# Attention's conversions and normalisation held in the source's order, row maxima transposed on VectorE, a fifth buffer of queries, and 44 expert groups in place of 46

## The chip, the cores and the metric

The kernel runs on one core of a Trainium2 chip. The metric is the device time of one launch in microseconds (us). A core has TensorE (PE; its weight loads are listed as PEld), VectorE (DVE), ScalarE (ACT), GpSimd (POOL) and SyncE (SP), which here only issues DMAs. Each engine takes its instructions in the order in which they stand in its stream. That order is not the order of the source: a planner chooses it before the program is built, by its own estimate of when each input is there, unless the source ties an instruction to the one before it on its engine.

## The reference

Two layers, 2048 tokens, width 1024. Each layer is a mixer, a layer norm, a mixture of experts and a layer norm. The first mixer is causal attention with 16 heads, whose scores have a part with 64 columns and a rotated part with 32; the second is a pooling mixer. Cut to what matters:

```
s = (q_nope @ k_nope.T + q_rope @ k_rope.T) * scale      # 16 heads, 64 + 32 columns
p = softmax(where(causal, s, -inf));  o = p @ v;  f = o @ w_o
x = layer_norm(alpha * x + f)
# experts: 64, two of them for each token, chosen within one of 8 groups
e = two of 64 per token, with gates
y[t] = sum over its two e of gate * (silu(x[t] @ w1[e]) * (x[t] @ w3[e])) @ w2[e]
x = layer_norm(alpha * x + y)
```

All is float32. The 4096 choices (two for each token) fall unevenly on the 64 experts.

## The kernel before

The stages follow each other: projections (queries, keys and values go to DRAM), attention, output projection with norm and routing, experts of layer 0, the pooling mixer with norm and routing, experts of layer 1, the last norm.

Attention works on pairs of heads `hp` (8) and blocks `b` of 512 queries (4). `run` goes through the steps (hp, b, k), k being a chunk of 128 keys: 40 steps for each pair of heads, two to a round, so 20 rounds. In a round stand, in this order: the scores of two steps (`scores`: ten matmuls for each into a PSUM tile `sc`, of which there are two; on the diagonal a mask added by VectorE at L906; then the exponential `pe` on ScalarE at L908), one item of maxima, the sums of the round before (`add`, one head on VectorE at L921, one on GpSimd at L922), the product with the values (`apply`, tile `po`), the steps of unfinished normalisations, a second item of maxima.

The maxima (`maxima`) run 24 items ahead of the scores. An item is four matmuls into the single PSUM tile `pm`, on the diagonal a mask on VectorE (L817), and a VectorE maximum (L819). After the last item of a (hp, b) the 128 x 8 maxima are turned by a TensorE transpose (L836) into a tile `sc`, negated by VectorE (L838), written to DRAM (`M`) and read from there into one row of each head's `qb` (two DMAs). The scores' matmuls add that row.

`finish` normalises a finished (hp, b): sums over the keys by a matmul into `sc`, two ScalarE copies `rl` and `o` (L865, L866), then through DRAM: sums out (L868), back as 128 x 8 (L871), reciprocal on VectorE (L874), out (L875), back spread over partitions (L878), product on GpSimd (L881), a split of `o` into two float32r halves `ot` (ScalarE L193, GpSimd L194), and a DMA to `OT` (L887). Each yield in it is one round.

`load_queries` brings a block of queries (one DMA for `qn`, L790, four for `qb`, L794) and splits both into two halves with `split` (ScalarE L193, GpSimd L194), after two ends of rounds (`behind`, `round`). There are four buffers of queries. `all_maxima` loads the next block when the maxima of one begin. `load_pair` brings keys (L776) and values.

`pin` ties an instruction behind the one that was traced before it on its engine. Before the change it is used for attention's matmuls, its masks, its maxima and VectorE's part of the sums. The exponentials, GpSimd's part of the sums, the splits, the copies of `finish`, the reciprocal and the DMAs are left to the planner.

The experts: a group is 128 rows in four blocks of 32 rows, each block of one expert. `groups` lays out which place (experts ranked by how many rows they have) gets how many blocks: 6 for places 0 to 2, 4 for 3 to 12, 3 for 13 to 36, 2 for 37 to 63, in all 46 groups, and `WORK` is their order. Rows over an expert's seats go to a loop at the end (`overflow`), run only when there are such rows. For each group a gather brings the rows, TensorE turns them (L1352), multiplies by w1 and w3 (L1364) and w2 (L1392), and a scatter writes them. The three matrices of an expert are 3 MB; `load_line` brings them on SP in the order of first use into five (layer 0) or six (layer 1) buffers, three of them during the stage before.

Of the kernel before, what the change touches and what calls it, by code (L numbers as in the profile page):

```python
# [20 lines left out]
P = 128  # L21
# [10 lines left out]
AT4, AT3, AT2 = 3, 13, 37  # L32
# [9 lines left out]
FIRST_AT = 6  # L42
LATE = -4
# [26 lines left out]
def groups():  # L70
# [3 lines left out]
    rests = [[(p, 4), (p, 5), (AT2 + p, 0), (AT2 + p, 1)] for p in range(AT4)]  # L74
    line = [(p, q) for p in range(AT3, AT2) for q in range(3)]
    threes = [line[i:i + NQ] for i in range(0, len(line), NQ)]
    line = [(p, q) for p in range(AT2 + AT4, NE) for q in range(2)]
# [5 lines left out]
    big = [[g] for g in range(n[1], n[2])] + [[g, n[2] + g] for g in range(n[1])]  # L83
    mid = [[g, g + 1, g + 2] for g in range(n[3], n[4], 3)]
    small = [[g] for g in range(n[4], n[5])]
    work = mid.pop(0)
    for i in range(len(big)):
# [3 lines left out]
    work += [g for part in (mid, small) for x in part for g in x]  # L91
    assert sorted(work) == list(range(len(every)))
# [10 lines left out]
def block_runs():  # L103
# [5 lines left out]
    for g, blocks in enumerate(GROUPS):  # L109
        for j, (p, q) in enumerate(blocks):  # L110
            kind = next(i for i, end in enumerate((AT3, AT2, AT2 + AT4, NE)) if p < end)
            found.setdefault((kind, j, q), []).append((p, g))
# [564 lines left out]
class Attention:  # L677


    def __init__(self, tc, c, QN, QR, K, KR, V, M, R, OT):  # L680
# [6 lines left out]
        self.acc, self.later, self.tails = {}, [], []  # L687
        self.ps = None
# [7 lines left out]
    def matmul(self, *a, **kw):  # L696
        return self.pin(self.nc.tensor.matmul(*a, **kw))  # L697

# [17 lines left out]
    def begin(self):  # L716
# [17 lines left out]
        for j in range(2):  # L734
            nc.gpsimd.memset(self.kb[j * DN + DR:j * DN + DR + 1].bitcast(F32), 1.0)
        self.new_keys(p0, 0)
        self.load_queries(0, 0)
        for b in range(NB - 1):
            self.load_pair(0, b)
            yield  # L740
            for _ in range(4 * (b + 1)):
                self.next_maxima()
# [7 lines left out]
    def load_rotated(self, b):  # L750
# [3 lines left out]
        raw = self.p0.tile([P, TB], F32, name="kraw")  # L754
# [3 lines left out]
        nc.gpsimd.tensor_tensor(raw, raw, self.ka[:, tb].bitcast(F32), op=ALU.subtract)  # L758
# [6 lines left out]
    def load_pair(self, hp, b):  # L765
# [11 lines left out]
        self.behind(lambda: split(nc, kt[:, 0, tb], kt[:, 1, tb], raw, nc.gpsimd))  # L777
# [3 lines left out]
    def load_queries(self, hp, b):  # L781
# [3 lines left out]
        qn = self.pq.tile([P, 2, TB], F32R, name="qn", bufs=4)  # L785
        qa = self.pq.tile([P, TB], F32R, name="qa", bufs=4)
        qb = self.pq.tile([P, TB], F32R, name="qb", bufs=4)
# [3 lines left out]
        self.behind(lambda: split(nc, qn[:, 0], qn[:, 1], raw, nc.gpsimd))  # L791
# [3 lines left out]
        self.behind(lambda: split(nc, qa, qb, rot, nc.gpsimd))  # L795

    def maxima(self, hp, b):
# [8 lines left out]
        for tt in range(4):  # L806
            for ch in range(b + 1):
# [18 lines left out]
    def next_maxima(self):  # L826
        tails, self.tails = self.tails, []
        next(self.maxima_of_all, None)
        for x in tails:
            x()  # L830

    def maxima_row(self, hp, b, mc):
        nc = self.nc
        qb = self.qs[hp, b][2]
        pt = (self.ps or self.psm).tile([P, 2, TB], F32, name="sc" if self.ps else "pm")[:, 0]
        self.pin(nc.tensor.transpose(pt[:8, :P], mc.rearrange("p j t -> p (j t)"), self.c.ident))  # L836
        mr = self.pq.tile([8, P], F32R, name="mr")
        self.pin(nc.vector.tensor_scalar(mr, pt[:8, :P], -1.0, None, op0=ALU.mult))  # L838
        nc.sync.dma_start(self.M[hp, b], mr.bitcast(F32))
        self.ready.add((hp, b))  # L840
        for j in range(2):
            r = j * DN + DR
            nc.sync.dma_start(qb[r:r + 1].bitcast(F32), self.M[hp, b, 4 * j:4 * j + 4].rearrange("t p -> (t p)").unsqueeze(0))

    def all_maxima(self):
        for i, x in enumerate(self.order):
            if 0 < i + 1 < len(self.order) and self.order[i + 1] != (0, NB - 1):
# [867 lines left out]
```

## Time and profile before

| | us |
|---|---|
| median of 3 runs (2955.05 to 2965.54) | 2963.32 |
| profiled execution, its own time | 2968.73 |
| span of its trace | 2966.5 |
| attention with maxima and scores alone, 375 to 1197 | 822 |
| experts of layer 0, 1447 to 2050 | 603 |
| experts of layer 1, 2282 to 2851 | 569 |

The projections end inside the first pairs of heads, so the stretch from 375 on is attention alone. In the page and in the trace's answers a group has the busy time and then the idle time of its engine just before it, with what ended that idle time. An arrow `<-` names the releaser.

### The profile page before, as it was taken

What the parts mean: (1) busy time and instruction counts of PE and PEld (TensorE: products, weight loads), DVE (VectorE), ACT (ScalarE), POOL (GpSimd) and SP (SyncE); (2) the same over time, 40 slices, a digit from 0 to 9 for tenths busy, and PEclk for the clock granted to TensorE, in tenths of its full rate; (3) what the DMA queues carried; (4) which work ended last, traced back from release to release, by engine and by line L of the source; (5) the groups of instructions that cost most, each with busy time, mean ns of one, the idle gap of its engine ahead of it and who ended that gap; (6) DMA issues with size and microseconds to landing.
All of it is one profiled execution on the core that took longest, in us unless ns stands there. A gap on an engine that the chain in (4) does not pass through costs nothing.

```text
span 2966.5 us, 50666 instructions
## 1 busy us (share of the span) xinstructions
PE 2657.1 (90%) x19378; PEld 1482.6 (50%) x19378; DVE 1454.7 (49%) x3675; ACT 823.2 (28%) x1433; POOL 897.4 (30%) x831
## 2 busy tenths in 40 slices
PE   6987989889898899999799999896996999999977
PEld 5874555555455555688533334332895333333323
DVE  7555767677677776455421111221896211111218
ACT  4444434434444434222111111111552111111102
POOL 4244656656565556200111111111111111111100
PEclk9998999999999999999899999998997999999988
DMA  6545122121221211647599999996756899999967
GB/s 202 194 154 172 55 65 80 58 72 55 80 65 55 72 37 56 190 147 240 194 385 418 409 415 403 370 419 217 209 174 272 334 419 417 412 412 412 414 259 291
DMA packets 230241, 690.21 MB, mean 233 GB/s; under 512 B 42318, under 2 KB 102990, under 8 KB 180588
## 3 DMA queue, kind: packets, MB, share of 16 engines
q1 hardware_dynamic: 189180, 577.62, 51.3%
q0 software_dynamic: 29408, 78.29, 7.8%
q10 hardware_dynamic: 11408, 31.02, 2.7%
q8 instruction: 155, 2.54, 0.3%
q14 instruction: 90, 0.74, 0.1%
HBM read 595.47 MB, written 120.71 MB: 241 GB/s over the span
## 4 chain that ended last, share of the span: by engine, by line
PE 57%; DMA 23%; DVE 12%; issue 3%; ACT 2%; POOL 1%; SPq 0%; ACTq 0%; DVEq 0%; POOLq 0%; another core or an unknown queue 0%
DMA w<-in_w_dram 15%; PE ph L1364 14%; PE sc L697 9%; PE po L697 6%; PE py L1392 6%; PE pz L1103 6%; PE pm L697 5%; DVE mx L819 3%; PE pt L1352 2%; PE pt L387 2%; PE pl L344 2%; PE plog L520 1%; PE pz L1244 1%; DMA R<-rl 1%; DMA qn<-QN 1%
## 5 line engine op out<-in xcount | busy, mean ns | idle before, releaser
L1364 PE MATMUL ph<-w,xT 128*32 128x512 f32 x5888 | 681.2, 602 | 39.3 <-DMA w<-in_w_dram 39.3
L1364 PEld LDWEIGHTS ph<-w,xT 128*32 128x32 f32 x5888 | 199.7, 111 | 447.6 <-issue 432.1
L819 DVE TENSOR_REDUCE mx<-pm 128x2 f32<-128x1024 f32 (+2 forms) x320 | 339.5, 1061 | 108.0 <-PE pm L697 102.7
L908 ACT ACTIVATE pe<-sc 128x1024 f32<-128x1024 f32 (+1 forms) x320 | 280.0, 895 | 367.1 <-DVE sc L906 211.0
L922 POOL TENSOR_TENSOR acc<-acc,pe 128x512 f32<-128x512 f32 (+3 forms) x256 | 311.8, 1218 | 218.5 <-ACT pe L908 210.2
L1321 POOL DMA_INDIRECT Y<-y,idst x92 | 92.3, 1003 | 936.7 <-ACT xT L1353 874.3
L1369 DVE SCALAR_TENSOR_TENSOR h<-sg,gate,ph 128x256 f32<-128x256 f32 x92 | 44.2, 481 | 657.5 <-ACT sg L1367 657.5
L1392 PE MATMUL py<-w,hT 128*32 128x512 f32 x2944 | 348.8, 592 | 1.6 <-DVE hT L1379 1.6
L697 PE MATMUL po<-pe,vt 128*64 128x512 f32 (+3 forms) x1280 | 283.0, 565 | 0.0
L697 PE MATMUL sc<-qn,k 64*128 64x512 f32 (+2 forms) x1920 | 260.5, 377 | 19.7 <-ACT rl L865 15.7
L921 DVE TENSOR_TENSOR acc<-acc,pe 128x512 f32<-128x512 f32 (+3 forms) x256 | 236.9, 925 | 11.0 <-ACT pe L908 10.0
L1367 ACT ACTIVATE sg<-ph 128x256 f32<-128x256 f32 x92 | 35.3, 383 | 719.3 <-PE ph L1364 707.2
L1392 PEld LDWEIGHTS py<-w,hT 128*32 128x32 f32 x2944 | 106.5, 110 | 214.2 <-issue 214.1
L697 PE MATMUL pm<-k,qn 64*128 64x512 f32 (+2 forms) x640 | 147.5, 454 | 71.2 <-DVE mx L819 65.3
L697 PEld LDWEIGHTS sc<-qn,k 64*128 64x128 f32 x1920 | 176.9, 194 | 65.3 <-ACT rl L865 20.9
L1394 DVE COPY y<-py 128x512 f32<-128x512 f32 x92 | 63.6, 692 | 224.4 <-PE py L1392 224.4
L697 PEld LDWEIGHTS pm<-k,qn 64*128 64x128 f32 x640 | 65.3, 196 | 192.4 <-DVE mx L819 97.7
L697 PEld LDWEIGHTS po<-pe,vt 128*64 128x64 f32 x1280 | 81.2, 142 | 134.7 <-issue 126.2
L1352 PEld LDWEIGHTS pt<-ident,xg 128*128 128x128 f32 x736 | 90.4, 194 | 97.9 <-issue 72.9
L1352 PE MATMUL pt<-ident,xg 128*128 128x128 f32 x736 | 108.3, 291 | 23.7 <-DMA xg<-X,isrc 22.4
L697 PE MATMUL pm<-ka,qa 64*128 64x512 f32 (+2 forms) x640 | 125.3, 383 | 0.3 <-ACT qa L193 0.3
L697 PE MATMUL sc<-qb,kb 33*128 33x512 f32 (+2 forms) x640 | 121.8, 372 | 0.0
(360 smaller groups left out, 4082.5 us busy)
## 6 DMA issues: line engine op xcount, KB each, us to landing
w<-in_w_dram SPq DMA_DIRECT2D x384, 1024.0 KB
fy<-Y SPq DMA_DIRECT2D x16, 1024.0 KB
OT<-ot SPq DMA_DIRECT2D x31, 512.0 KB
K<-kq SPq DMA_DIRECT2D x32, 256.0 KB
V<-v SPq DMA_DIRECT2D x16, 512.0 KB
QN<-kq SPq DMA_DIRECT2D x32, 256.0 KB
qn<-QN SPq DMA_DIRECT2D x32, 256.0 KB
qb<-QR SPq DMA_DIRECT2D x128, 64.0 KB
```

Source lines behind the costliest of these rows:

```text
L344: nc.tensor.matmul(pl, a[:, k, :], w[:, k, :], start=(k == 0 and n == 0), stop=(k == ND - 1 and n == 2))
L697: return self.pin(self.nc.tensor.matmul(*a, **kw))
L819: self.pin(nc.vector.tensor_reduce(mx[:, :, tt, ch], pm[:, :, :n], axis=AX.X, op=ALU.max))
L908: nc.scalar.activation(pe[:, :, c0:], sc[:, :, c0:], AF.Exp, scale=SCALE)
L921: self.pin(self.nc.vector.tensor_tensor(acc[:, 0, c0:], before[:, 0, c0:], pe[:, 0, c0:], op=ALU.add))
L922: self.nc.gpsimd.tensor_tensor(acc[:, 1, c0:], before[:, 1, c0:], pe[:, 1, c0:], op=ALU.add)
L1103: nc.tensor.matmul(pz, o[:, a, k, :], wo.parts[k][b][:, hs], start=(n == 0), stop=(n == 3 * ND - 1))
L1321: st = self.nc.gpsimd.indirect_dma_start(out=self.Y, out_offset=bass.IndirectOffsetOnAxis(ap=idx, axis=0), in_=y, in_offset=None, bounds_c ...
L1352: self.pin(nc.tensor.transpose(pt[:, j, :], x[:, half * 4 + j, :], self.c.ident))
L1364: self.pin(nc.tensor.matmul(ph[js], xT[:, k, js], w[:, :, k, :], start=(k == 0), stop=(k == ND - 1), tile_position=(0, j * n)))
L1392: self.pin(nc.tensor.matmul(py[js], hT[:, k, js], w[:, k, hs], start=(k == 0), stop=(k == NF - 1), tile_position=(0, j * n)))
L1394: (nc.vector.tensor_copy if half else nc.scalar.copy)(y[:, hs], py)
```

## The change

- In attention, the splits, the copies, the reciprocal and the product of `finish` are pinned too (`split` of the class, L865, L866, L874, L881). The exponentials, GpSimd's part of the sums and all DMAs are not.
- The maxima are no longer turned on TensorE. VectorE negates them into eight columns of a 128 x 32 tile and transposes that in 32 x 32 blocks; eight DMAs of 4 x 32 elements for each (hp, b) write the rows of `qb` straight from SBUF. The DRAM tile `M` is no longer used. The step `next_maxima`, which did the turning one item later, goes.
- A fifth buffer of queries (in the pool `p1`, for every fifth block), and each block from the second pair of heads on is loaded eight items of maxima ahead of its first use.
- `finish` keeps `o` in the second half of `ot`, with three buffers of `ot` and none of `o`. The rotated keys are loaded into the place of the split keys in place of a tile of their own.
- The experts' places get 6 blocks (place 0), 5 (1 and 2), 4 (3 to 12), 3 (13 to 34), 2 (35 to 59) and 1 (60 to 63): 44 groups. `WORK` starts with the same four groups; the experts with the most rows come at the 5th, 8th and 14th group in place of the 34th, 40th and 42nd; the last group holds the last two places.

```diff
-AT4, AT3, AT2 = 3, 13, 37
+AT5, AT4, AT3, AT2, AT1 = 1, 3, 13, 35, 60
+AHEAD = 8
...
+    def split(self, hi, lo, src):
+        self.pin(self.nc.scalar.copy(hi, src))
+        self.pin(self.nc.gpsimd.tensor_tensor(lo, src, hi.bitcast(F32), op=ALU.subtract))
...
-        self.behind(lambda: split(nc, kt[:, 0, tb], kt[:, 1, tb], raw, nc.gpsimd))
+        self.behind(lambda: self.split(kt[:, 0, tb], kt[:, 1, tb], raw))
...
+        pool, bufs = (self.p1, 1) if self.order.index((hp, b)) % 5 == 4 else (self.pq, 4)
...
-                    self.tails.append(lambda: self.maxima_row(hp, b, mc))
+                    mr, mt = self.mr, self.pq.tile([P, 32], F32R, name="mt")
+                    self.pin(nc.vector.tensor_scalar(mr[:, 0:8], mc.rearrange("p j t -> p (j t)"), -1.0, None, op0=ALU.mult))
+                    self.pin(nc.vector.transpose(mt.bitcast(F32), mr.bitcast(F32)))
+                    self.ready.add((hp, b))
+                    for j in range(2):
+                        row = qb[j * DN + DR:j * DN + DR + 1].rearrange("o (t q c) -> o t q c", t=4, q=4)
+                        for q in range(4):
+                            e = 32 * q + 4 * j
+                            nc.sync.dma_start(row[:, :, q].bitcast(F32), mt[e:e + 4].bitcast(F32))
...
+            for _ in self.maxima(*x):
+                while waiting and items >= waiting[0][0]:
+                    self.load_queries(*waiting.pop(0)[1])
+                items += 1
+                yield
...
-            nc.scalar.copy(rl, pl)
-            nc.scalar.copy(o, po)
+            self.pin(nc.scalar.copy(rl, pl))
+            self.pin(nc.scalar.copy(o, po))
...
-            nc.vector.reciprocal(r8, r8)
+            self.pin(nc.vector.reciprocal(r8, r8))
...
-            nc.gpsimd.tensor_tensor(o, o, rl, op=ALU.mult)
+            self.pin(nc.gpsimd.tensor_tensor(o, o, rl, op=ALU.mult))
```

## Rows read from the trace of the kernel before

**Rows 1.** The page's first part: busy time, share of the span and instructions of each engine.

```profile
PE 2657.1 (90%) x19378; PEld 1482.6 (50%) x19378; DVE 1454.7 (49%) x3675; ACT 823.2 (28%) x1433; POOL 897.4 (30%) x831
```

**Rows 2.** Busy time by stage: the stretch, its length, busy time of each engine with its instructions, then the granted clock, the DMAs' share and GB/s. Attention, the experts of layer 0, the experts of layer 1.

```profile
375.00:1197.00 822.00, 730.18 (x5160) 425.89 (x5156) 586.67 (x817) 336.24 (x443) 493.83 (x413) 0.95 0.21 63
...
1447.00:2050.00 603.00, 565.27 (x4943) 215.10 (x4943) 122.59 (x265) 73.52 (x140) 95.35 (x108) 0.96 0.93 379
2282.00:2851.00 569.00, 542.64 (x4755) 200.91 (x4755) 101.56 (x203) 71.21 (x136) 90.32 (x89) 0.98 0.95 386
```

**Rows 3.** Groups of instructions in attention, 375 to 1197: busy us and mean ns, then the engine's idle time just before and its releasers.

```profile
L697 PE MATMUL sc<-qn,k 64*128 64x512 f32 (+2 forms) x1702 | 230.5, 376 | 17.8 <-ACT rl L865 15.7 <-ACT pe L908 1.8
...
L697 PE MATMUL pm<-k,qn 64*128 64x512 f32 (+2 forms) x520 | 118.0, 448 | 50.2 <-DVE mx L819 49.4
...
L836 PE MATMUL sc<-ident,mc 128*8 128x128 f32 x26 | 7.5, 289 | 23.6 <-ACT pe L908 23.6
L838 DVE TENSOR_SCALAR mr<-sc 8x128 fp32r<-8x128 f32 x26 | 7.1, 273 | 0.5
L874 DVE RECIPROCAL r<-r 128x8 f32<-128x8 f32 x28 | 5.6, 200 | 44.9 <-DMA r<-R 44.9
L822 DVE TENSOR_REDUCE mc<-mx 128x8 f32<-128x32 f32 x26 | 4.8, 186 | 0.9
```

**Rows 4.** Who waited for whom, 400 to 1180: us in total, times, longest.

```profile
ACT ot L193 <- POOL o L881: 68.7, 27, 4.1
...
DVE r L874 <- DMA r<-R: 44.9, 22, 5.5
...
ACT qn L193 <- DMA qn<-QN: 29.6, 16, 4.5
```

**Rows 5.** TensorE in order of time, the instructions that begin after an idle time, which stands in brackets with its releaser: first and last of the seven long waits for L819 (421.51 and 1130.24), and a period of one pair of heads between two of them (779.67 to 898.64) with its other waits.

```profile
421.51 0.80 PE L697 MATMUL pm<-k,qn 64*128 64x512 f32 x2 [4.38 <-DVE mx L819]
...
779.67 0.79 PE L697 MATMUL pm<-k,qn 64*128 64x512 f32 x2 [4.66 <-DVE mx L819]
...
868.25 0.27 PE L836 MATMUL sc<-ident,mc 128*8 128x128 f32 x1 [1.99 <-ACT pe L908]
...
878.42 0.97 PE L697 MATMUL sc<-qn,k 64*128 64x512 f32 x6 [2.27 <-ACT rl L865]
...
898.64 0.80 PE L697 MATMUL pm<-k,qn 64*128 64x512 f32 x2 [4.69 <-DVE mx L819]
...
931.71 0.27 PE L836 MATMUL sc<-ident,mc 128*8 128x128 f32 x1 [1.68 <-ACT pe L908]
...
1130.24 0.80 PE L697 MATMUL pm<-k,qn 64*128 64x512 f32 x2 [2.86 <-DVE mx L819]
```

**Rows 6.** VectorE in order of time: the reciprocal ahead of the wait at 898.64.

```profile
897.29 0.20 DVE L874 RECIPROCAL r<-r 128x8 f32<-128x8 f32 x1 [5.13 <-DMA r<-R]
```

**Rows 7.** ScalarE in order of time, ahead of the wait at 878.42.

```profile
877.26 0.62 ACT L193 CAST qn<-qn 128x512 fp32r<-128x512 f32 x1 [4.50 <-DMA qn<-QN]
877.79 0.58 ACT L865 COPY rl<-sc 128x512 f32<-128x512 f32 x1
```

**Rows 8.** SP's DMA issues in order of time: the queries' load of Rows 7, and the two DMAs that bring a row of maxima.

```profile
871.95 0.45 SPq L790 DMA_DIRECT2D qn<-QN  x1
...
874.30 1.09 SPq L843 DMA_DIRECT2D qb<-M  x2
```

**Rows 9.** Busy time by stretches of 10 us with the columns of Rows 2: the stretches of the first, the fifth and the last of the seven long waits, and an undisturbed one.

```profile
415.00:425.00 10.00, 5.62 (x38) 3.79 (x36) 5.26 (x10) 1.75 (x3) 2.25 (x2) 0.76 0.28 80
...
895.00:905.00 10.00, 6.36 (x34) 4.06 (x36) 6.60 (x9) 1.05 (x3) 2.16 (x3) 0.66 0.25 79
...
1125.00:1135.00 10.00, 7.14 (x48) 4.20 (x46) 6.37 (x11) 2.60 (x4) 2.81 (x3) 0.83 0.21 63
...
945.00:955.00 10.00, 10.00 (x70) 5.46 (x67) 5.93 (x10) 5.30 (x6) 5.99 (x6) 1.00 0.10 29
```

**Rows 10.** Busy time by stretches of 20 us in the experts' stages, columns as in Rows 2.

```profile
2300.00:2320.00 20.00, 19.34 (x179) 7.87 (x175) 4.91 (x12) 3.11 (x6) 3.33 (x4) 1.00 0.49 185
...
2340.00:2360.00 20.00, 20.00 (x184) 7.41 (x180) 3.91 (x7) 2.14 (x4) 4.06 (x4) 1.00 1.02 420
...
2820.00:2840.00 20.00, 20.00 (x186) 6.83 (x177) 3.06 (x6) 2.52 (x5) 0.99 (x1) 1.00 0.51 211
...
2020.00:2040.00 20.00, 20.00 (x188) 6.71 (x181) 3.22 (x6) 2.14 (x4) 1.94 (x2) 1.00 0.30 107
```

**Rows 11.** The groups of w1 and w3's matmuls in the experts of layer 1 (2294 to 2852) and of layer 0 (1462 to 2046), columns as in Rows 3.

```profile
L1364 PE MATMUL ph<-w,xT 128*32 128x512 f32 x2884 | 332.7, 601 | 15.1 <-DMA w<-in_w_dram 15.1
...
L1364 PE MATMUL ph<-w,xT 128*32 128x512 f32 x2944 | 342.1, 604 | 24.1 <-DMA w<-in_w_dram 24.1
```

**Rows 12.** The chain that ended last in the experts of layer 1, start and length: the w1 and w3 matmuls of the last two groups, and the w2 matmuls after the second of them.

```profile
2829.11 7.00 PE ph L1364 x64
...
2840.88 7.00 PE ph L1364 x64
2847.88 3.50 PE py L1392 x32
```

**Rows 13.** SP's last issues of expert matrices, layer 1 and layer 0.

```profile
2816.05 3.15 SPq L1305 DMA_DIRECT2D w<-in_w_dram  x2
...
2022.23 0.33 SPq L1305 DMA_DIRECT2D w<-in_w_dram  x1
```

More of the change, by code (lines that the diff above doesn't have):

```diff
@@ L82, in groups @@
         n.append(n[-1] + len(x))
-    big = [[g] for g in range(n[1], n[2])] + [[g, n[2] + g] for g in range(n[1])]
-    mid = [[g, g + 1, g + 2] for g in range(n[3], n[4], 3)]
+    big = [[g, n[2] + g] for g in range(n[1])] + [[g] for g in range(n[1], n[2])]
+    mid = [list(range(g, min(g + 3, n[4]))) for g in range(n[3], n[4], 3)]
     small = [[g] for g in range(n[4], n[5])]
     work = mid.pop(0)
-    for i in range(len(big)):
+    i = 0
+    while big or mid or small:
         for part in (small, big, mid if i % 3 == 1 else []):
@@ L90, in groups @@
                 work = work + part.pop(0)
-    work += [g for part in (mid, small) for x in part for g in x]
-    assert sorted(work) == list(range(len(every)))
+        i += 1
+    assert sorted(work) == list(range(len(every))) and all(len(x) == NQ for x in every)
     return every, work
@@ L110, in block_runs @@
         for j, (p, q) in enumerate(blocks):
-            kind = next(i for i, end in enumerate((AT3, AT2, AT2 + AT4, NE)) if p < end)
+            kind = next(i for i, end in enumerate((AT3, AT2, AT2 + AT4, AT1, AT1 + AT4 - 1, NE)) if p < end)
             found.setdefault((kind, j, q), []).append((p, g))
@@ L790, in load_queries @@
         nc.sync.dma_start(raw, self.QN[2 * hp:2 * hp + 2, :, tb].rearrange("h d t -> (h d) t"))
-        self.behind(lambda: split(nc, qn[:, 0], qn[:, 1], raw, nc.gpsimd))
+        self.behind(lambda: self.split(qn[:, 0], qn[:, 1], raw))
         rot = qb.bitcast(F32)
@@ L794, in load_queries @@
             nc.sync.dma_start(rot[i * DR:(i + 1) * DR], self.QR[2 * hp + i // 2, :, tb])
-        self.behind(lambda: split(nc, qa, qb, rot, nc.gpsimd))
+        self.behind(lambda: self.split(qa, qb, rot))
     def maxima(self, hp, b):
@@ L846, in all_maxima @@
+                yield
+    def all_maxima(self):
+        items, waiting, at = 0, [], 0
+        for hp, b in self.order:
+            if (hp, b) > (0, NB - 1):
+                waiting.append((at - AHEAD, (hp, b)))
+            at += 4 * (b + 1)
         for i, x in enumerate(self.order):
-            if 0 < i + 1 < len(self.order) and self.order[i + 1] != (0, NB - 1):
+            if 0 < i + 1 < NB - 1:
                 self.load_queries(*self.order[i + 1])
-            yield from self.maxima(*x)
+            for _ in self.maxima(*x):
[3 more added lines that the diff above has]
+                yield
@@ L969, in run @@
             ended = [g for g in done if g]
-            self.next_maxima()
+            next(self.maxima_of_all, None)
             if before:
```

58 lines of the change are left out of this document (21 added, 37 removed).

## The prediction

> **What bounds the kernel now.** I read the page's first part, then the busy time by stage. TensorE is busy for 90% of the span [rows 1]. The two stretches that the change touches are bound differently. In attention TensorE works 730.18 of 822 us with the DMAs at a share of 0.21: what is to be won there is the 91.8 us in which it stands still and the half speed that follows (granted clock 0.95). In the experts the DMAs run at 0.93 and 0.95 beside TensorE's 565 of 603 and 543 of 569 us: two limits nearly level [rows 2].
>
> Third, the groups of attention: nearly all of TensorE's idle time has three direct causes. It waits 49.4 us for VectorE's maximum L819, 23.6 us for ScalarE before a turn of maxima L836, 15.7 us for the copy L865 [rows 3]. The direct cause is not the root, so I went one step back along the waits. VectorE stood 44.9 us before the reciprocal L874, for a DMA; ScalarE stood 29.6 us before splits of queries for theirs, and 68.7 us before splits of outputs for GpSimd [rows 4]. One period of a pair of heads shows it in place. TensorE waits 4.69 us at 898.64 for L819 [rows 5]; ahead of that maximum VectorE had put a reciprocal whose data were still on their way, and stood 5.13 us [rows 6]. It waits 2.27 us at 878.42 for the copy L865 [rows 5]; the copy stood on ScalarE behind a split of queries that waited 4.50 us [rows 7]. The planner, which is free to place these, took the DMAs to be sooner than they are. A period is 898.64 - 779.67 = 119.0 us [rows 5], a round a twentieth of it, 5.95 us.
>
> **The change, part by part.** *The reciprocal.* In the source it stands two rounds, 11.9 us, behind the issue of its load; the standing load took at most 5.5 us of VectorE's time [rows 4]. Pinned there it no longer waits. Seven of TensorE's waits for L819 are of this kind, 4.38 us the first, 2.86 the last [rows 5], 31.0 us together; the other 18 us of that row are half microseconds where TensorE and VectorE alternate on the single tile `pm`, and stay. Behind each of the seven the granted clock drops: 0.76, 0.66, 0.83 in the 10 us around the first, fifth and last, 1.00 in a stretch without such a wait [rows 9], that is the lower level, 1.2 GHz, for part of them. Summed over the seven, (1 - clock) x 10 us is 17.9 us; part of it lies in the wait itself, so I take half, 9. Together 40, bounds 20 (half the waits come back elsewhere) and 49.
>
> *ScalarE's and GpSimd's order, and the earlier queries.* The splits now stand one to two rounds behind their load, and the load stands eight items, four rounds or 24 us, ahead of the first use, in a buffer that the scores left at least eight items before (distance five in place of four). The load of rows 7 was issued at 871.95 [rows 8] and there at 877.26 [rows 7], 5.3 us later. The split of an output stands a round behind GpSimd's product, so the 68.7 us go too, which cost TensorE only where a copy stood behind. Of the 15.7 us I take 12, bounds 0 and 15.7. GpSimd does the same instructions in another order: nothing.
>
> *The transpose.* On TensorE 26 turns go, 7.5 us busy, and the 23.6 us before them [rows 3]. Not all is won: the turn waited for a tile `sc`, and the scores that come next need it too. What stood between, the values' product, now goes first. Where VectorE is full (at 868.25, where the exponential waited for a mask behind sums and maxima) that wins little; where the values' product was ready (at 931.71) it wins the 1.68 us [rows 5]. I take half the idle time, 12, and 5 of the 7.5: 17, bounds 0 and 31. VectorE loses the negation from PSUM, 273 ns, and gets one from SBUF and a 128 x 32 transpose. No such transpose is in the trace. The nearest row, the maximum over the same 128 x 32, takes 186 ns [rows 3]; at 186 for each of the two VectorE does 0.1 us more for each (hp, b), 3 us in 32, beside a VectorE that works 587 of 822 us: nothing, bounds 0 and 3. SP issues eight DMAs in place of three, each about half of the 1.09 us of a pair [rows 8]: 2.7 us more for each (hp, b), which delays what is queued behind on SP, sums of `finish` and loads of keys among them. All have a round or more in hand, and the row itself is needed 24 items, 71 us, later. Nothing; without that cover 2.7 us of SP each time, 87 at most.
>
> *The rest.* The keys' own tile, the merged `o` and `ot`: their dependencies move by less than the buffers' slack. Two more steps in `counts` and three more small matmuls between stages: under 1 us.
>
> Attention: 40 + 12 + 17 = 69, say 70 us, out of a ceiling of 91.8 idle and 41 of half speed (0.05 x 822 [rows 2]).
>
> *The experts.* The last two groups' matmuls begin 11.77 us apart [rows 12]; two groups fewer in two layers are 47 us of TensorE. But the matrices, 3 MB for each of 64 experts, and the rows gathered and scattered stay the same, and between 2340 and 2820 they keep the DMAs full, at a share of 1.02 and 420 GB/s [rows 10]: this stream does not go faster. (The Trainium skill, "DMA: Bandwidth & Descriptors", section Where 436 GB/s comes from, gives 435 GB/s as the ceiling of the ports into SBUF; the trace agrees, within 4%.) So what can be won is what TensorE still does once the last matrices are there. SP issues the last at about 2818 [rows 13]; the DMAs fall to 0.51 in the next 20 us [rows 10], so they land near 2830, and TensorE ends at 2851.4 [rows 12]. In the new order the last group holds the last two places, so TensorE still has the end of that group's w1 and w3 and its w2 to do, 4 to 12 us behind the landing. That ends 2834 to 2842, 9 to 17 us sooner, taken 12. In layer 0 the last issue is at 2022.2 [rows 13], the DMAs stand at 0.30 [rows 10] and TensorE ends near 2045, by the same working 6 to 14 us, taken 8. TensorE waited for matrices 15.1 and 24.1 us [rows 11]; those waits grow by what is not won. Sum 20, bounds 0 (the start of the stage, at a DMA share of 0.49 [rows 10] because buffers were full, gets longer) and 35.
>
> Seats: 192, 2 x 160, 10 x 128, 22 x 96, 25 x 64 and 4 x 32. Ranking the reference's own inputs as the kernel does, every expert fits; the tightest, place 60 of layer 1, has 32 rows for 32 seats. So `overflow` runs no turn.
>
> **Sum.** 2968.7 - 70 - 20 = 2878.7 against the profiled execution, which lies 5.4 us over the median of the runs; against the median 2873 us.
>
> **The rivals.** (A) *VectorE becomes attention's bound.* For: it is busy 71% over the whole stretch, and with TensorE on one tile `pm` every late maximum is a wait; at 868 it was full. Against: at the long waits it was itself standing still [rows 6]. Then half of the 70 come back as shorter waits for L819: 2963 - 35 - 12 = 2916.
> (B) *The pinned order stalls ScalarE, and the kernel is slower.* Now 16 splits in a period stand at fixed places, and what the planner put behind them must wait when a DMA is late: exponentials are queued behind, scores wait for their tile `sc`, values for `pe`. SP still issues in the planner's order, where a load of queries can stand behind a DMA that waits. A stall cost TensorE 2.27 us [rows 5] for 4.50 of ScalarE's [rows 7]. Against the 90 us won it decides from 90 / 2.27 = 40 stalls, six of the 16 in each of seven periods. Against: four rounds of lead. With eight in each period it is 127 - 90 = 37 slower, 3000.
> (C) *The experts give nothing*, because the stream of matrices starts and ends where it did: 2893.
> (D) *Nearly all idle time of attention goes*, with its clock: 110 there and 30 in the experts, 2823.
> (E) *It does not do what it says:* exponentials, sums on GpSimd and DMAs are not pinned, and the planner moves the same waits to them: 20 from the experts remain, 2943.
>
> **How the numbers follow.** The forecast, with 2845 to 2888 around it, has 0.43. (A) 0.2, (B) 0.08, (C) 0.12, (D) 0.12, (E) 0.05. The range reaches from (D) at its lower bound to the low ends of attention (28 us) and the experts (0): 2818 to 2935. It leaves out (B), (E) and some of (D). A run of this kernel can tell 0.5%, 15 us, from no change: faster by more is all but (B) and a part of (E), 0.87; within 0.05; slower 0.08.
>
> **What would show it.** Right: in attention the reciprocal's wait near zero, no row L836, L865 and the split `qn` without waits for DMAs, granted clock near 1.00, a period of 105 to 110 us; in the experts 44 groups, TensorE's waits for matrices longer than before, its end within 12 us of the last landing. Wrong: waits of ScalarE for `qn<-QN` or `k<-K` in every period (B); L819's row still at 40 us or more with VectorE busy ahead of it (A); a stretch from the first group to the last as long as before (C). The whole is wrong if the attention stretch shrinks by less than 30 us.

## The result and the profile after

The changed kernel takes 2883.54 us (median of 4 runs, 2880.15 to 2892.98), the kernel before 2964.43 beside it: a ratio of 0.9723, 95% interval 0.9704 to 0.9742, 81 us. Forecast were 2873 us and a range of 2818 to 2935. The profiled execution took 2881.38 us, its span is 2879.3.

Both profiles, cut at the same five points (starts and ends of TensorE's instructions in order of time), show where the 87.2 us of span went. The last column is the forecast.

| | before | after | difference | forecast |
|---|---|---|---|---|
| to the last sums over the keys (end of attention) | 1198.25 | 1124.65 | -73.6 | -70 |
| to the first w1/w3 matmul, layer 0 | 265.5 | 269.8 | +4.3 | 0 |
| to TensorE's last w2 matmul, layer 0 | 586.0 | 576.4 | -9.7 | -8 |
| to the first w1/w3 matmul, layer 1 | 244.8 | 245.1 | +0.4 | 0 |
| to TensorE's last w2 matmul, layer 1 | 572.6 | 558.3 | -14.3 | -12 |
| to the end | 99.4 | 105.0 | +5.6 | 0 |

A single profile places a stage only to some us: with the 44 groups alone, attention's code is that of the kernel before, and its profile shows it 7.8 us shorter.

The sum is right, and that hides that several of its terms are not. First the stages of the changed kernel (stretch, length, busy time of each engine with its instructions, granted clock, DMA share, GB/s), against [rows 2]:

```profile
375.00:1124.00 749.00, 696.70 (x5158) 411.56 (x5154) 594.97 (x847) 334.29 (x449) 520.44 (x419) 1.00 0.25 69
1394.00:1971.00 577.00, 543.93 (x4670) 205.26 (x4668) 113.63 (x229) 69.95 (x134) 87.96 (x100) 0.97 0.94 384
2215.00:2774.00 559.00, 540.04 (x4672) 201.93 (x4670) 98.73 (x194) 69.66 (x133) 85.08 (x84) 0.98 0.96 392
```

In attention the same work fits into 749 us in place of 822. TensorE stands still for 749 - 696.7 = 52.3 us in place of 91.8, and it is busy 33.5 us less, of which 7.5 are the turns of [rows 3] that are gone; the rest goes with the granted clock, 1.00 in place of 0.95. The groups of that stretch, in the columns of [rows 3]:

```profile
L698 PE MATMUL sc<-qn,k 64*128 64x512 f32 (+2 forms) x1706 | 221.5, 363 | 0.0
L698 PE MATMUL pm<-k,qn 64*128 64x512 f32 (+2 forms) x524 | 115.3, 434 | 50.0 <-DVE mx L828 49.0
...
L833 DVE TENSOR_SCALAR mr<-mc 128x8 fp32r<-128x8 f32 x26 | 8.1, 310 | 0.9
L834 DVE STREAM_TRANSPOSE mt<-mr 128x32 f32<-128x32 f32 x26 | 5.5, 212 | 2.7 <-DVE mr L833 1.4
L884 DVE RECIPROCAL r<-r 128x8 f32<-128x8 f32 x28 | 5.3, 191 | 0.0
```

The reciprocal's 44.9 us are gone, the scores wait for nothing, the turns and their 23.6 us don't exist. But the wait for VectorE's maximum (now L828) is as large as it was, 49.0 us. It is made of other pieces. One period of a pair of heads (714.12 to 820.90, 106.8 us in place of 119.0), TensorE's instructions that begin after more than 0.6 us of idle time:

```profile
714.12 0.50 PE L698 MATMUL pm<-k,qn 64*128 64x512 f32 x2 [1.45 <-DVE mx L828]
...
756.40 0.39 PE L698 MATMUL pm<-k,qn 64*128 64x256 f32 x2 [0.65 <-DVE mx L828]
...
767.92 0.39 PE L698 MATMUL pm<-k,qn 64*128 64x256 f32 x2 [1.32 <-DVE mx L828]
...
770.55 0.49 PE L698 MATMUL pm<-k,qn 64*128 64x512 f32 x2 [0.94 <-DVE mx L828]
...
789.99 0.50 PE L698 MATMUL pm<-k,qn 64*128 64x512 f32 x2 [1.05 <-DVE mx L828]
```

Ahead of the last of these, VectorE and GpSimd in order of time:

```profile
784.80 1.23 DVE L828 TENSOR_REDUCE mx<-pm 128x2 f32<-128x1024 f32 x1
...
785.72 1.30 POOL L702 TENSOR_TENSOR k<-k 128x512 fp32r<-128x512 f32 x1
...
786.06 0.19 DVE L831 TENSOR_REDUCE mc<-mx 128x8 f32<-128x32 f32 x1
...
786.28 0.76 DVE L833 TENSOR_SCALAR mr<-mc 128x8 fp32r<-128x8 f32 x1
...
786.98 1.28 POOL L931 TENSOR_TENSOR acc<-acc,pe 128x512 f32<-128x512 f32 x1
...
787.08 0.21 DVE L834 STREAM_TRANSPOSE mt<-mr 128x32 f32<-128x32 f32 x1
787.21 1.59 DVE L930 TENSOR_TENSOR acc<-pe 128x512 f32<-128x512 f32 x1
...
788.72 1.21 DVE L828 TENSOR_REDUCE mx<-pm 128x2 f32<-128x1024 f32 x1
```

From 784.80 on VectorE has no gap here. The negation L833 is eight columns wide and yet takes 0.76 us; in 14 of its 26 executions it took 0.17. It ends where GpSimd's instruction ends (787.04 and 787.02). The forecast had it at 0.19 us, under other work.

### The profile page after: what moved, and what is told of

Read it like the earlier page. It is cut to its first block, busy times and chain, and to the rows that moved or that the text cites. A ratio compares the mean times of both kernels' runs of the same rounds, so it can differ in the third digit from the quotient of the medians.

```text
span 2879.3 us, 50088 instructions
## 1 busy us (share of the span) xinstructions
PE 2591.7 (90%) x18934; PEld 1460.6 (51%) x18934; DVE 1452.1 (50%) x3699; ACT 810.8 (28%) x1421; POOL 910.4 (32%) x824
## 4 chain that ended last, share of the span: by engine, by line
PE 53%; DMA 25%; DVE 15%; issue 4%; SPq 1%; ACT 1%; POOL 1%; DVEq 0%; POOLq 0%; ACTq 0%
DMA w<-in_w_dram 20%; PE ph L1373 11%; PE sc L698 8%; PE po L698 6%; PE pz L1112 6%; PE pm L698 5%; PE py L1401 5%; DVE mx L828 5%; PE pl L346 2%; PE pt L389 2%; PE pt L1361 2%; DVE acc L930 1%; PE plog L522 1%; PE pz L1253 1%; DVE pm L826 1%
## 5 line engine op out<-in xcount | busy, mean ns | idle before, releaser
L1373 PE MATMUL ph<-w,xT 128*32 128x512 f32 x5632 | 667.7, 610 | 48.4 <-DMA w<-in_w_dram 48.2
L828 DVE TENSOR_REDUCE mx<-pm 128x2 f32<-128x1024 f32 (+2 forms) x320 | 339.6, 1061 | 90.2 <-PE pm L698 85.2
L931 POOL TENSOR_TENSOR acc<-acc,pe 128x512 f32<-128x512 f32 (+3 forms) x256 | 305.9, 1195 | 137.0 <-ACT pe L917 127.3
L1401 PE MATMUL py<-w,hT 128*32 128x512 f32 x2816 | 338.6, 592 | 1.7 <-DVE hT L1388 1.7
L698 PE MATMUL po<-pe,vt 128*64 128x512 f32 (+3 forms) x1280 | 273.2, 548 | 0.0
L698 PE MATMUL sc<-qn,k 64*128 64x512 f32 (+2 forms) x1920 | 250.6, 365 | 0.8 <-ACT kq L395 0.8
L930 DVE TENSOR_TENSOR acc<-acc,pe 128x512 f32<-128x512 f32 (+3 forms) x256 | 228.3, 892 | 8.2 <-ACT pe L917 7.1
L698 PE MATMUL pm<-k,qn 64*128 64x512 f32 (+2 forms) x640 | 143.9, 442 | 73.6 <-DVE mx L828 65.4
```

Of the source, the lines that this page charges most:

```text
L828: self.pin(nc.vector.tensor_reduce(mx[:, :, tt, ch], pm[:, :, :n], axis=AX.X, op=ALU.max))
L930: self.pin(self.nc.vector.tensor_tensor(acc[:, 0, c0:], before[:, 0, c0:], pe[:, 0, c0:], op=ALU.add))
L931: self.nc.gpsimd.tensor_tensor(acc[:, 1, c0:], before[:, 1, c0:], pe[:, 1, c0:], op=ALU.add)
L1373: self.pin(nc.tensor.matmul(ph[js], xT[:, k, js], w[:, :, k, :], start=(k == 0), stop=(k == ND - 1), tile_position=(0, j * n)))
L1401: self.pin(nc.tensor.matmul(py[js], hT[:, k, js], w[:, k, hs], start=(k == 0), stop=(k == NF - 1), tile_position=(0, j * n)))
```

## The experiments

Each ratio below is against runs of the kernel before on the same chip; versions of different sets are compared by their ratios, and a thousandth is 3 us. The rows are from 375 to 1100 us. A `...` in an edit stands for lines of it that are not shown.

**Two parts alone.** The kernel before with only the reciprocal pinned, and with only the 44 groups.

```diff
-            nc.vector.reciprocal(r8, r8)
+            self.pin(nc.vector.reciprocal(r8, r8))
```

> The kernel before, with one edit: the reciprocal of the normalisation (L874) is pinned behind what was traced before it on VectorE. Theory one (each stall goes with the pin that causes it, as forecast): VectorE's 44.9 us before the reciprocal go, and with them the seven long waits of TensorE, 31 us, and 9 us of half speed: attention 40 us shorter, 2924 us. Theory two, from the trace after the change, in which TensorE stands still for only 39 us less but works 33 us less for the same products: the clock that falls behind each long wait is worth twice that, 18 us: attention 49 shorter, 2915 us, granted clock of attention 0.97 or more. Rival (the waits only move to the turns L836 and the copies L865): 15 us or less, 2950 us, and L836's and L865's idle time grows by some 20 us.

```diff
-AT4, AT3, AT2 = 3, 13, 37
+AT5, AT4, AT3, AT2, AT1 = 1, 3, 13, 35, 60
...
```

> The kernel before with the layout of 44 expert groups alone; attention as before. Forecast theory (the end comes 4 to 12 us behind the last matrices): the experts' stages 8 and 12 us shorter, 2944 us. Theory from the trace after the change (TensorE still has several groups in hand when the last matrices land, since the last seven groups ask for only ten experts): 10 and 3 us shorter, and the last norm some 5 us shorter because its first inputs find free tiles earlier, 2946 us. Rival (TensorE sets the stages): 47 us shorter, 2917 us. What sets the experts apart from the last norm is each stage's length in the trace.

The reciprocal alone: 2950.74 us, ratio 0.9956 [0.9939, 0.9972], 13 us in place of the 40 forecast. The groups of TensorE show why:

```profile
L697 PE MATMUL sc<-qn,k 64*128 64x512 f32 x1512 | 202.1, 373 | 32.0 <-ACT rl L865 31.5 <-ACT pe L908 0.4
L697 PE MATMUL pm<-k,qn 64*128 64x512 f32 (+2 forms) x504 | 112.2, 440 | 21.9 <-DVE mx L819 20.4
```

The long waits for L819 did go (20.4 us are left of 44.8 in the same stretch, which holds six of the seven), but the wait for the copy L865 doubled, from 15.7 to 31.5: ScalarE's stalls were next in line. The rival's number came (15 us or less, 2950 us), and the waits moved as it had them, but to L865 alone: L836's stay at 20.5 us (21.6 before). The granted clock of the stretch rose from 0.95 to 0.97.

The groups alone: 2946.15 us, ratio 0.9945 [0.9927, 0.9963], 16 us of the 20 forecast. Cut as above, the experts of layer 0 take 576.2 us and those of layer 1 558.9, which is 9.8 and 13.7 less, and the last norm 103.3, which is 3.9 more. That is the changed kernel's picture again. The theory from the trace had 10 and 3, and a shorter norm: it is wrong in layer 1 and in the norm.

**The transposition taken back.** The changed kernel with TensorE's turns, the negation from PSUM and the way through DRAM.

```diff
-                    self.pin(nc.vector.tensor_scalar(mr[:, 0:8], mc.rearrange("p j t -> p (j t)"), -1.0, None, op0=ALU.mult))
-                    self.pin(nc.vector.transpose(mt.bitcast(F32), mr.bitcast(F32)))
...
+                    self.tails.append(lambda: self.maxima_row(hp, b, mc))
...
```

> The kernel after with the maxima turned on TensorE again, through a score tile, VectorE's negation and DRAM, all else as after (pins, five buffers, 44 groups). Forecast theory: 17 us slower than after, 2901 us, with waits of TensorE before L836's turn of about 1.8 us each again. Rival (VectorE is full there, so the wait for a score tile only takes the place of a wait for the maximum): 5 us or less slower, 2888 us, the waits for the maximum shrinking by what the turns wait.

2868.91 us, ratio 0.968 [0.9664, 0.9696]: 13 to 15 us faster than the change, where both theories had it slower. The turns' waits are back, as forecast (21.5 us), but the wait for the maxima falls by more, from 49.0 to 19.7, and the negation from PSUM costs what it cost before:

```profile
L699 PE MATMUL pm<-k,qn 64*128 64x512 f32 (+2 forms) x522 | 114.9, 435 | 20.8 <-DVE mx L827 19.7
...
L844 PE MATMUL sc<-ident,mc 128*8 128x128 f32 x26 | 7.1, 273 | 21.5 <-ACT pe L926 21.5
...
L846 DVE TENSOR_SCALAR mr<-sc 8x128 fp32r<-8x128 f32 x26 | 7.1, 274 | 0.4
```

So the part "transposition", as changed, is a loss. Which of its pieces is at fault, the last set tells.

**The pins and the lead.** Four versions of the changed kernel: the reciprocal unpinned; of the new pins only the reciprocal's kept; four buffers of queries at the same lead; four buffers and the old moment of loading.

```diff
-            self.pin(nc.vector.reciprocal(r8, r8))
+            nc.vector.reciprocal(r8, r8)
```

> The changed kernel with one pin taken away: the reciprocal of the finish goes back to the planner; splits, copies, product, transposes, buffers and groups as changed. Pinning the reciprocal alone in the kernel before brought 12 us, not the 40 forecast. Theory 1 (joint: both stalls stand on one chain, finish by ScalarE, GpSimd and VectorE, so that it takes both pins to shorten a period): the reciprocal's wait comes back with some 30 us of idle time and TensorE's granted clock falls under 0.98 in attention; 25 to 50 us slower than the changed kernel, 2908 to 2933. Theory 2 (the splits and copies in source order did it all; with them the planner places the reciprocal well itself): within 5 us of the changed kernel.

```diff
-        self.pin(self.nc.scalar.copy(hi, src))
-        self.pin(self.nc.gpsimd.tensor_tensor(lo, src, hi.bitcast(F32), op=ALU.subtract))
+        self.nc.scalar.copy(hi, src)
+        self.nc.gpsimd.tensor_tensor(lo, src, hi.bitcast(F32), op=ALU.subtract)
...
-            self.pin(nc.scalar.copy(rl, pl))
-            self.pin(nc.scalar.copy(o, po))
+            nc.scalar.copy(rl, pl)
+            nc.scalar.copy(o, po)
...
-            self.pin(nc.gpsimd.tensor_tensor(o, o, rl, op=ALU.mult))
+            nc.gpsimd.tensor_tensor(o, o, rl, op=ALU.mult)
```

> The changed kernel with the reciprocal pinned, but the splits' copies (ScalarE) and subtractions (GpSimd), and the finish's copies and product, given back to the planner; transposes, the fifth buffer, loads eight rounds ahead and groups stay. Theory 1 (joint): ScalarE and GpSimd again stand behind a query's or a key's DMA while a finish waits; ScalarE's waits for queries and keys come back (more than 30 us between 375 and 1125 us), with waits of the finish's copy, and the kernel takes 25 to 50 us more than the changed one. Theory 2 (the early loads alone empty these waits, since a transfer issued eight rounds ahead has landed whatever the order): within 6 us.

```diff
-        pool, bufs = (self.p1, 1) if self.order.index((hp, b)) % 5 == 4 else (self.pq, 4)
+        pool, bufs = self.pq, 4
```

> The kernel after with four buffers of queries in place of five, loads still placed eight items ahead, so a load can wait on SP's queue for a buffer that the scores still read. Theory one (the pinned order needs the fifth buffer): splits of queries stand on ScalarE for late loads once or twice in each period, 2 to 5 us each, which hold the exponentials up: 12 to 37 us slower than after, 2896 to 2920 us. Rival (the pins alone do it; the buffer is free early enough): within 3 us of after, 2884 us, no waits of ScalarE for a load of queries.

The fourth has that edit too, and this one:

```diff
...
-            for _ in self.maxima(*x):
-                while waiting and items >= waiting[0][0]:
-                    self.load_queries(*waiting.pop(0)[1])
-                items += 1
-                yield
+            yield from self.maxima(*x)
```

> The changed kernel with the loading of queries of the kernel before: four buffers, a block loaded when the maxima of the block before it begin, in place of eight items ahead of its own; the pinned splits stand where that puts them, two ends of rounds behind the load. Theory B (rival B of the prediction: the pinned order stalls ScalarE when a load is late): waits of ScalarE for queries over 40 us between 375 and 1125, and 20 to 60 us more than the changed kernel. Theory L (a load two rounds ahead is enough for a 5 us transfer; the lead only keeps the buffer's release out of the way): within 10 us of the version with four buffers, 2880 to 2900.

| changed kernel with | us | ratio | interval |
|---|---|---|---|
| reciprocal unpinned | 2907.25 | 0.98 | 0.9773 to 0.9826 |
| of the new pins only the reciprocal's | 2971.24 | 1.0035 | 1.0012 to 1.0057 |
| four buffers | 2889.59 | 0.9754 | 0.9734 to 0.9774 |
| four buffers, old loading | 2922.22 | 0.9867 | 0.984 to 0.9893 |

Reciprocal unpinned, its own row and the one behind it:

```profile
L884 DVE RECIPROCAL r<-r 128x8 f32<-128x8 f32 x26 | 5.2, 199 | 35.4 <-DMA r<-R 35.4
...
L698 PE MATMUL pm<-k,qn 64*128 64x512 f32 (+2 forms) x522 | 116.2, 438 | 72.2 <-DVE mx L828 70.3
```

The stall is back, with 21 us more of waiting for TensorE and a clock of 0.98 in place of 1.00, and the price is 23 us, a little under the 25 to 50 of theory 1. Only the reciprocal pinned:

```profile
L698 PE MATMUL sc<-qn,k 64*128 64x512 f32 (+2 forms) x1434 | 199.4, 384 | 34.5 <-ACT rl L875 27.5 <-ACT pe L917 6.9
...
L701 ACT CAST ot<-ot 128x512 fp32r<-128x512 f32 x24 | 14.9, 619 | 91.9 <-POOL ot L891 91.9
L701 ACT CAST qn<-qn 128x512 fp32r<-128x512 f32 x24 | 14.8, 618 | 47.0 <-DMA qn<-QN 47.0
```

ScalarE's waits are all back, even for queries that are loaded eight items ahead (47.0 us, more than before; the expectation's eight rounds should read eight items, which is four rounds): ScalarE waits in the splits, and TensorE for the copy L875 behind them, as in [rows 7]. The price is 88 us by the medians, 92 by the ratios, far above the 25 to 50 of theory 1; without these pins the rest of the change brings nothing (ratio 1.0035). The stretch 375 to 1100, of the changed kernel and of this version, in the columns of [rows 2]:

```profile
375.00:1100.00 725.00, 674.96 (x5008) 400.14 (x5006) 579.89 (x831) 324.37 (x438) 500.14 (x404) 1.00 0.26 70
```
```profile
375.00:1100.00 725.00, 634.66 (x4404) 370.26 (x4404) 527.67 (x743) 287.26 (x385) 426.11 (x362) 0.94 0.22 65
```

TensorE stands still 40 us longer, and the clock of 0.94 is worth about as much again (an estimate: 0.06 x 725 = 44 us). The edit frees ScalarE's and GpSimd's instructions together, so which of the two engines' pins matter was not told apart.

Four buffers at the same lead cost 6 to 9 us, with intervals that just overlap, so neither theory's number came: ScalarE does wait 34.4 us for queries, but TensorE only 2.4 for the exponentials. With the old loading it is 39 to 43, by ScalarE's waits and TensorE's for the exponentials. The two versions in this order, the first with its row of ScalarE alone:

```profile
L701 ACT CAST qn<-qn 128x512 fp32r<-128x512 f32 x25 | 15.6, 623 | 34.4 <-DMA qn<-QN 34.4
```
```profile
L701 ACT CAST qn<-qn 128x512 fp32r<-128x512 f32 x25 | 15.4, 617 | 56.9 <-DMA qn<-QN 56.9
...
L698 PE MATMUL sc<-qn,k 64*128 64x512 f32 (+2 forms) x1536 | 206.8, 375 | 20.8 <-ACT pe L908 20.7
```

That is rival B's mechanism in the place where the prediction put it, pinned and no lead, and theory B's numbers (over 40 us of waits, 20 to 60 us more). Rival B's own price, 3000 us, did not come: this version is still faster than the kernel before.

**The negation.** The changed kernel with negation and transposition one item later, so that the next maximum no longer stands behind them; the same without the negation; the same with a second reduction in the negation's place; and without the negation, the transposition in its old place. The new row of -1 takes the negation's part in the product.

```diff
-                    self.pin(nc.vector.tensor_scalar(mr[:, 0:8], mc.rearrange("p j t -> p (j t)"), -1.0, None, op0=ALU.mult))
-                    self.pin(nc.vector.transpose(mt.bitcast(F32), mr.bitcast(F32)))
...
+                    self.tails.append(lambda: self.maxima_row(hp, b, mc))
...
```

The new `maxima_row` holds both instructions and the DMAs, one item later.

> The changed kernel with the negation and the 32x32 transposition of a block's maxima placed one item of the maxima later in VectorE's order, so that the next maximum no longer stands behind them. Theory A (in the diagonal rounds VectorE is full, so each operation ahead of a maximum holds TensorE's next maxima by its own length plus the wait of the transposition for the negation): the waits behind the maxima shrink by 0.4 to 0.9 us at each of 32 blocks after the first pair, 8 to 20 us in all: 2864 to 2876. Theory B (VectorE's total in the round decides, not its order; only operations taken off it help, as where TensorE turned them): within 4 us of the changed kernel. Theory C (the row's DMAs start later and the products that read it wait): slower by 5 us or more.

```diff
-            nc.gpsimd.memset(self.kb[j * DN + DR:j * DN + DR + 1].bitcast(F32), 1.0)
+            nc.gpsimd.memset(self.kb[j * DN + DR:j * DN + DR + 1].bitcast(F32), -1.0)
...
-                    mc = self.pq.tile([P, 2, 4], F32, name="mc")
+                    mc = self.mr[:, 0:8].rearrange("p (j t) -> p j t", j=2)
...
-        self.pin(nc.vector.tensor_scalar(mr[:, 0:8], mc.rearrange("p j t -> p (j t)"), -1.0, None, op0=ALU.mult))
```

> As the one before, and the negation is gone: the constant row of the keys that the maxima's row is multiplied with holds -1 in place of 1, and the reduction writes the maxima straight into the tile that is transposed. VectorE has 32 operations of 310 ns (8 to 10 us of its own time) less. Theory A (order): no more than 3 us on top of the late placement, since the negation already stands where VectorE has room. Theory B (VectorE's total decides): 5 to 10 us below the changed kernel with the late placement worth nothing by itself. Both together, 2855 to 2870, would stand at or under the version with TensorE's turns (2869).

```diff
...
+        self.pin(nc.vector.tensor_reduce(mc, mx, axis=AX.X, op=ALU.max))
         self.pin(nc.vector.transpose(mt.bitcast(F32), mr.bitcast(F32)))
```

> The version without negation and with the late transposition (2853.5), with one more VectorE instruction in the place where the late negation stood: the last reduction over a block's maxima, 128 x 8 from 128 x 32, is done a second time ahead of the transposition and writes the same values. It takes 0.18 to 0.19 us in the changed kernel whether GpSimd works beside it or not; the negation took 0.17 us alone and up to 0.77 beside GpSimd, and placed late up to 2.4. Theory P (the negation was dear because it waits for GpSimd, as the sums on VectorE do): the same count of instructions on VectorE as with the late negation, but only 32 times 0.2 us more, 2854 to 2861. Theory N (one more dependent instruction in the place, of whatever kind, costs the 30 us): back to 2876 to 2886.

> The changed kernel without the negation (the constant row of the keys holds -1, and the reduction writes straight into the tile that is transposed), the transposition left in its place ahead of the next maximum. It tells what the late placement is worth by itself once the negation is gone. Theory A (order matters in the full rounds: transposition ahead of a maximum holds TensorE): 10 us of the 30 stay, 2866 to 2876. Theory B (only the negation counted, by its waits for GpSimd and its 0.2 us to the next instruction): 2850 to 2860.

| | us | ratio | interval | end of attention |
|---|---|---|---|---|
| changed kernel | 2883.54 | 0.9723 | 0.9704 to 0.9742 | 1124.65 |
| late, with negation | 2883.64 | 0.9729 | 0.9706 to 0.9753 | 1126.81 |
| late, no negation | 2853.5 | 0.9622 | 0.9598 to 0.9645 | 1105.32 |
| late, a reduction in its place | 2854.5 | 0.9636 | 0.9609 to 0.9662 | 1100.88 |
| in place, no negation | 2858.26 | 0.9655 | 0.9628 to 0.9683 | 1102.75 |

Placed late, the negation got dearer, from 310 ns in the mean to 800; without it, the wait for the maxima is 16 us smaller than the change's. The negation of the first version, the second reduction of the third, and TensorE's wait in the fourth:

```profile
L845 DVE TENSOR_SCALAR mr<-mc 128x8 fp32r<-128x8 f32 x26 | 20.8, 800 | 0.0
```
```profile
L845 DVE TENSOR_REDUCE mr<-mx 128x8 fp32r<-128x32 f32 x26 | 4.5, 172 | 0.0
```
```profile
L698 PE MATMUL pm<-k,qn 64*128 64x512 f32 (+2 forms) x520 | 113.7, 431 | 35.7 <-DVE mx L828 33.5 <-PE sc L698 0.9
```

And the late negation's longest execution, with GpSimd's instruction beside it:

```profile
683.14 2.38 POOL L196 TENSOR_TENSOR woL<-ot,woH 128x1024 fp32r<-128x1024 f32 x1
683.15 2.40 DVE L845 TENSOR_SCALAR mr<-mc 128x8 fp32r<-128x8 f32 x1
```

It began 0.01 us behind GpSimd and ended 0.03 us behind it. The reduction in the same place, reading 128 x 32, took 172 ns in the mean and cost nothing that the runs can tell (theory P); theory N's 30 us did not come. Order by itself is worth nothing that these runs can tell: late against in place is 2853.5 against 2858.26 with overlapping intervals. (The ends of attention do not decide it: the late version's profiled execution took 2859.82 us, 6 over its median.) My first two theories, order and VectorE's total, both had the size wrong (3 and 5 to 10 us for 30). What was missing is that the kind of instruction counts: this one gets longer beside GpSimd, the reduction does not. VectorE's total is not it: it is busy 593 us of attention from 375 on with the second reduction and 595 in the changed kernel, 29 us apart in time.

That does not yet give the size. In the changed kernel the 26 negations take 8.1 us in all, 3.7 of them over the 0.17 that each takes alone, and without them TensorE waits some 16 us less for the maxima. How the one grows into the other was not followed. Placed late, part of the price is the clock: 0.98 from 375 to 1100 us, against 1.00 in the three versions without the negation.

The version without the negation, transposing late, has the lowest median: 2853.5 us, 110 us under the kernel before. Its interval lies wholly under those of the change and of TensorE's turns, but overlaps with those of the other two versions without the negation.

## Why the prediction was right, and where it was not

The time was right by luck: a term too low by far (ScalarE's order) and two too high (the reciprocal, the transposition) cancelled. The stalls that it named did go; what each was worth was not as forecast.

*The reciprocal, 40.* The wait went as forecast and so did 24 us of L819's row, but the gain was 13 us alone, under the lower bound of 20, and 23 on top of the rest, just over it. The step that failed is "31.0 us together" taken as won: TensorE then waits 16 us more for the copies L865, which VectorE's stalls had covered. (With one pin more the planner may also place the rest otherwise; that was not compared.)

*ScalarE's and GpSimd's order and the earlier queries, 12 with an upper bound of 15.7.* The worst step. Taking the pins away costs 88 to 92 us, the lead and the buffer 39 to 43. From the parts, the order with the lead is worth about 81 - 13 - 16 + 14 = 66 us in the changed kernel (total, less the reciprocal, less the groups, plus the transposition's loss); that is a remainder, not a measurement. I had bounded it by TensorE's direct wait in the kernel before, which is no bound: with the reciprocal's stall gone the same wait was 31.5 us, and without the pins half of the price is the clock. Two stalls that cover each other are worth little one by one, and the bounds for each must hold for both gone. Why the taken-back pins cost 88 and the sum of the parts leaves 66 is open: the new dependencies of `ot` and of the buffers, in the planner's hands, may be the difference, but that part was not tried by itself.

*The transposition, 17.* Without the negation it is worth, against TensorE's turns and by the ratios, 0.968 - 0.9655 or 7 us in place, with intervals that overlap, and 0.968 - 0.9622 or 17 late, the forecast's size at best. The step that failed is "VectorE does 0.1 us more for each (hp, b) ... nothing, bounds 0 and 3". The negation costs 20 to 25 us in place and 30 late, and the part became a loss of 13 to 15. The sentence costed it by an instruction (the reduction, 186 ns) that does not get longer beside GpSimd: negation and transposition together took 522 ns, not 372, and what TensorE lost by it was more than the difference in VectorE's time.

*The clock, 9 of those 40.* TensorE's busy time fell by 33.5 us, of which 7.5 are the turns: 26 by the clock, which is at its upper level for nearly all of the stretch (of 15 stretches of 50 us from 375 on, 13 have a granted clock of 1.00 and two of 0.97). I had counted only the 10 us behind seven waits, and halved that. The reciprocal's pin alone moves the clock from 0.95 to 0.97, and its loss in the changed kernel from 1.00 to 0.98: about 14 us of 725 either way, by these rounded clocks. The rest is not told apart.

*The experts, 20.* 16 alone; in the changed kernel 9.7 and 14.3, with 5.6 given back in the last norm. TensorE's waits for matrices grew, as forecast, from 24.1 to 30.9 us in layer 0 and from 15.1 to 17.3 in layer 1. The size is right, the working of the end is not. In the changed kernel, TensorE's end, the last issues of matrices and those of X on SP:

```profile
2747.97 7.07 PE L1373 MATMUL ph<-w,xT 128*32 128x512 f32 x64
...
2758.85 7.07 PE L1373 MATMUL ph<-w,xT 128*32 128x512 f32 x64
2765.74 3.62 PE L1401 MATMUL py<-w,hT 128*32 128x512 f32 x32
...
2770.62 3.64 PE L1401 MATMUL py<-w,hT 128*32 128x512 f32 x32 [0.83 <-DVE hT L1388]
```
```profile
2738.83 3.01 SPq L1314 DMA_DIRECT2D w<-in_w_dram  x2
2755.09 11.18 SPq L1667 DMA_DIRECT2D w<-X  x5
...
2770.26 4.88 SPq L1667 DMA_DIRECT2D w<-X  x5
```
```profile
2720.00:2740.00 20.00, 20.00 (x184) 7.40 (x180) 4.39 (x8) 2.94 (x6) 1.99 (x2) 1.00 1.02 412
2740.00:2760.00 20.00, 20.00 (x184) 6.77 (x180) 3.70 (x7) 2.52 (x5) 0.98 (x2) 1.00 0.77 309
```

The last matrices are issued 522.9 us behind the first matmul of the layer (2215.91), as before (521.6): rival C was right about the stream. With 309 GB/s in the next 20 us, some of them for X, I estimate the landing at 2750. TensorE ends at 2774.3, 24 us later, not 4 to 12: when the last matrices land, it has only just begun the w1 and w3 of the last group but one (2747.97). And in the kernel before TensorE did not end at 2851.4, as I read from [rows 12]: there the chain passes to SP, and TensorE still does the w1 and w3 of one more group and the w2 of two:

```profile
2851.68 7.07 PE L1364 MATMUL ph<-w,xT 128*32 128x512 f32 x64
2858.57 3.62 PE L1392 MATMUL py<-w,hT 128*32 128x512 f32 x32
...
2863.45 3.64 PE L1392 MATMUL py<-w,hT 128*32 128x512 f32 x32 [0.83 <-DVE hT L1379]
```

It ends at 2867.1, 37 us behind the landing that the prediction estimated at 2830. Both ends were misread by some 15 us, which cancelled. I put the 5.6 us of the last norm down to this end, without a run that tries it: before, all ten loads of X were issued from 2852.22 on, beside TensorE's last 15 us; now five are issued only at 2770.26, 4 us ahead of its end.

*At nothing:* the output projection got 4.3 us longer. Over all versions of the change that stretch is between 263.3 and 270.5 us, in no order that the edits explain; why is open.

*The rivals.* (A) came in part: L828's row stayed at 49 us with VectorE busy ahead of it, the sign that the prediction gave. Its price of 35 is near the negation's 20 to 30, but the cause is not VectorE's share of busy time: with the second reduction in the negation's place VectorE is busy 592.6 of 725 us, in the changed kernel 579.9, and the kernel is 29 us faster. (B) was kept off by the lead. (C) was right about the stream but not about the stages, which got shorter. (D) and (E) did not come.

## What to carry to other kernels

Where several engines stall in the same stretch, take the stalls as one term: one pin alone moves the wait to the next engine, and a bound read from the direct wait is good only while the other stall stands. Before a cheap instruction is put on VectorE, look at the spread of its kind's durations, not the mean, and at what GpSimd does at that moment; a sign or a constant factor may go into an operand that is already there. The point where the chain leaves an engine is not that engine's end.

## What the runs showed of the hardware

On VectorE, some kinds of instruction get longer while GpSimd works. In the changed kernel between 375 and 1100 us, the 18 sums `acc<-acc,pe` of 128 x 512 with GpSimd idle took 0.67 to 0.68 us each, the 127 beside a GpSimd instruction 1.09 in the mean and up to 1.72. The negation took 0.17 us alone and up to 0.77 beside GpSimd, up to 2.40 placed late. The maximum from PSUM (1.22 us), the small reduction (0.19) and the transposition (0.21) were the same with and without. The trace shows this as a longer instruction, not as idle time, so no row of waits names it.

The Trainium skill, "SBUF — State Buffer", section SBUF: two separate sides, says that GpSimd and VectorE share a pair of ports that one of them holds for a whole instruction, on VectorE's side for instructions with two SBUF inputs or in a mode that uses both ports. The durations agree for the sums, which have two inputs in SBUF, and for the small reduction, which has one and doesn't wait. The negation has one input too, and waited (2.40 us beside 2.38); that it runs in a mode that uses both ports is the reading that fits, and no run here shows the mode. The Trainium skill, "VectorE: DVE Perf Modes", section The three transpose paths, puts VectorE's transposition of 128 x 128 in bf16 ahead of TensorE's (311 against 390 ns). Here, with other shapes and float32, 212 ns for 128 x 32 stand against 289 for the turn [rows 3]: the order agrees, and it was not what decided.
